# A hybrid diffusion layer: the FFN's up projection with both halves of its input in one 512-column operand

## The chip, the cores and the metric

The kernel runs on one core of a Trainium2 chip. The metric is the device time of one execution in microseconds; for the kernel before it is the median of three runs.

## The reference

One layer works on 256 latent tokens and 256 context tokens, 2048 channels wide, in fp32. The first part (modulated norm, one combined input projection, windowed attention and gated linear attention, merge, output projection) is not touched by the change. The second part is a ConvFFN with 5632 hidden channels:

```python
def conv_ffn(h, w_up, conv_w, conv_b, w_down):
    T = h.shape[1]
    u = h @ w_up
    up = jnp.pad(u, ((0, 0), (CONV_W // 2, CONV_W // 2), (0, 0)))
    u = sum(up[:, j:j + T] * conv_w[j] for j in range(CONV_W)) + conv_b
    a, g = jnp.split(u, 2, axis=-1)
    return (jax.nn.silu(a) * g) @ w_down

x = x + mod_x[5] * conv_ffn(modulate(x, g_ffn[l], mod_x[3], mod_x[4]),
                            w_up[l], conv_w[l], conv_b[l], w_down[l])
```

`mod_x[5]` is a gate row, silu(c) times a 2048 x 2048 part of `w_mod`; the kernel computes it in the background of the up projection.

## The kernel before, in words

**Products in three parts.** Every fp32 operand of a large product is split into a high part, rounded to fp32r (`whi`, `h2h`, `ah`), and the rest (`wlo`, `h2l`, `al`). A product is the sum of three: high x high, high x low and low x high, all added up in one PSUM region. `split` (L60) does it with an ACT copy (L61) and a DVE subtraction (L62).

**Weights.** They come in blocks of 256 rows x 512 columns (two k tiles of 128), loaded by SP's queue into seven `raw` buffers (L152) and split into three `whi` and three `wlo` buffers (L159, L160). The split is issued at high priority, so it stands ahead of other work in the queues of ACT and DVE.

**Order.** The instructions are not run in the order in which the code emits them: a planner, when the program is built, lays out each engine's queue from priorities, buffers that come free and its own estimate of durations. On the chip each engine then works through its queue in that order.

**Up projection** (L911 to L936). The 5632 hidden channels are taken in 11 blocks of 512, six in half 0 and five in half 1; after each half the down projection takes what is there. Each block has two sides (the two halves of `w_up`'s columns), each side one `proj_T` of 8 steps of two k tiles. In a step PE does 24 matmuls of 256 columns (the tokens): with weights `whi` 16, each column tile and k tile once with `h2h` (L203) and once with `h2l` (L206), and with `wlo` 8 with `h2h` (L203 again). Two column tiles share a bank, so a side takes two of the four banks of the pool `acc`, and the next side the other two. At the end of a side `up_evac` reads the banks: ACT scales by the middle tap and adds the bias (L923), DVE adds the two neighbours' taps (L924, L926), straight out of PSUM; side 0 goes through silu (L929), side 1 is multiplied with it (L931) and split into `ah` and `al` for the down projection.

**The input** `h2h`, `h2l` is made just before: per k tile DVE scales `x1T` (L376), ACT adds the shift and rounds (L377), DVE subtracts (L378).

**The other four banks** are the pool `ps`: one `main` and three `side`. Transposes and small products elsewhere in the kernel use them.

**Background work.** `tick()` runs at the head of each step of a projection. It counts down deferred work (`defer(n, fn)`: fn is emitted at the first tick at which its count falls below zero) and runs background steps at a rate: in half 0 it is 0.36 steps a tick, 32 steps in all. Each is two DVE multiply-adds of a `w_mod` block into `macc` (L264, L266); its block shares the seven `raw` buffers and SP's queue with the weights. Every eighth step ends a sum: a transpose and a reduction on DVE (L270, L272), then, deferred by three ticks, a little matmul `pcl` into the `main` bank (L276), copies out of it and the bias (L280, L282) into `gcol2`. After half 0's blocks `rows_from_cols` turns `gcol2` into the gate row: a PE transpose (L291), an ACT copy, a store to DRAM and a load spread over all partitions (L297, POOL's queue).

**Down projection** (`proj_nat`, L941 to L953): per 512 output columns the two token tiles are the stationary operands and the weights move, 512 columns a matmul (L176, L177, L181); `dn_evac` multiplies with the gate row (L945) and adds.

Of the kernel before, what the change touches and what calls it, by code (L numbers as in the profile page):

```python
# [8 lines left out]
F32 = mybir.dt.float32  # L9
F32R = mybir.dt.float32r  # L10
# [6 lines left out]
P = 128  # L17
# [13 lines left out]
def layer_kernel(ctx, tc, A, out):  # L31
# [18 lines left out]
    def M(name, shape, dt=F32):  # L50
        return big.tile(shape, dt, name=name, tag="M")
# [4 lines left out]
    def bank(name, shape=(P, 512), side=False):  # L56

        return ps.tile(list(shape), F32, name=name, tag="side" if side else "main", bufs=3 if side else 1)
# [66 lines left out]
    def defer(n, fn):  # L125

        later.append([n, fn])

    def flush():
        while later:  # L130
            later.pop(0)[1]()

    def tick():

        for e in later:
            e[0] -= 1
        while later and later[0][0] < 0:
            later.pop(0)[1]()
        if beside:
            beside[2] += beside[1]  # L140
            while beside[2] >= 1.0:
                beside[2] -= 1.0
                next(beside[0], None)
        bg_rate[1] += bg_rate[0]
        while bg_rate[1] >= 1.0 and bg_steps:
            bg_rate[1] -= 1.0
            bg_steps.pop(0)()
# [37 lines left out]
    def proj_T(w, c0, kts, rhs, evac):  # L185

        n = len(rhs)
        per = 2 // n
        banks = [acc.tile([P, 512], F32, name="acc", tag="acc") for _ in range(4 // per)]
        for k0 in kts[::2]:  # L190
            tick()
            nk = min(2, kts[-1] + 1 - k0)
            hi, lo = wsplit(w[k0 * P:(k0 + nk) * P, c0:c0 + 512])
            for part in range(2):
                for f in range(4):
                    for k in range(nk):
                        kt = k0 + k
                        w_ = (lo if part else hi)[:, k, f * P:(f + 1) * P]
                        for i, r in enumerate(rhs):
                            b = (f % per) if n == 1 else i  # L200
                            o = banks[f // per][:, b * T:(b + 1) * T]
                            ahi, alo = r(kt)
                            PE.matmul(o, w_, ahi, start=(kt == kts[0] and b == 0 and part == 0),  # L203
                                      stop=(kt == kts[-1] and part == 1), skip_group_check=True)
                            if part == 0:
                                PE.matmul(o, w_, alo, start=False, stop=False, skip_group_check=True)  # L206
        for i in range(len(banks)):
            evac(i, banks[i])

    ALL = list(range(KT))  # L210


# [26 lines left out]

        return [lambda k0=k0: step(k0) for k0 in range(0, KT, nk)]  # L240

    def mod_latent(parts):


        seq = [(part, dst, j, k0) for part, dst in parts for j in range(4) for k0 in range(0, KT, 2)]
        raws, a = {}, []

        def get(i):
            if i < len(seq) and i not in raws:
                part, _, j, k0 = seq[i]  # L250
                c0 = part * D + j * 512
                raws[i] = wload(w_mod[k0 * P:k0 * P + 256, c0:c0 + 512])

        def step(i):
            part, dst, j, k0 = seq[i]
            get(i)
            get(i + 1)
            if k0 == 0:
                a[:] = [W2("mod", "macc", [P, 512])]
            raw = raws[i]  # L260
            for k in range(2):
                kt = k0 + k
                if kt == 0:
                    V.tensor_scalar(a[0], raw[:, 0, :], ccol[:, 0:1], None, op0=ALU.mult)  # L264
                else:
                    V.scalar_tensor_tensor(a[0], raw[:, k, :], ccol[:, kt:kt + 1], a[0],  # L266
                                           op0=ALU.mult, op1=ALU.add)
            if k0 == KT - 2:
                tr = W2("mod", "mtr", [P, 16, 32])
                V.transpose(tr.rearrange("p a c -> p (a c)"), a[0])  # L270
                rs = sm.tile([P, 16], F32, name="mrs", tag="mrs", bufs=2)
                V.tensor_reduce(rs, tr, op=ALU.add, axis=AX.X)  # L272

                def out():
                    pc = bank("pcl", (32, 16))
                    PE.matmul(pc, sel[:, 0:32], rs, start=True, stop=True)  # L276
                    pv = pc.rearrange("p (a b) -> p b a", b=4)
                    d = dst[:, 4 * j:4 * j + 4]
                    for b4 in range(4):
                        V.tensor_copy(d[32 * b4:32 * b4 + 32, :], pv[:, b4, :])  # L280
                    b0 = part * 16 + j * 4
                    V.tensor_tensor(d, d, bmod[:, b0:b0 + 4], op=ALU.add)  # L282

                defer(3, out)

        return [lambda i=i: step(i) for i in range(len(seq))]

# [86 lines left out]
    def affine_split(hi, lo, xk, row, scale, shift):  # L374

        V.scalar_tensor_tensor(xk, xk, scale, row, op0=ALU.mult, op1=ALU.mult)  # L376
        S.activation(hi, xk, AF.Identity, bias=shift)  # L377
        V.scalar_tensor_tensor(lo, xk, shift, hi.bitcast(F32), op0=ALU.add, op1=ALU.subtract)  # L378
# [518 lines left out]
    r1 = rms_scale(s1, D, [P, 2])  # L897
    V.scalar_tensor_tensor(scale2, scale2, 1.0, gffn, op0=ALU.add, op1=ALU.mult)
    rrow = token_rows("fb", "rrow", r1)
    h2h = [M(f"h2h{i}", [P, 8, T], F32R) for i in range(2)]  # L900
    h2l = [M(f"h2l{i}", [P, 8, T], F32R) for i in range(2)]
    for kt in range(KT):
        xk = x1T[kt // 8][:, kt % 8, :]
        affine_split(h2h[kt // 8][:, kt % 8, :], h2l[kt // 8][:, kt % 8, :], xk, rrow,
                     scale2[:, kt:kt + 1], shift2[:, kt:kt + 1])
    bg_steps.extend(mod_latent([(5, gcol2)]))
    bg_rate[:] = [0.36, 0.0]
    h2 = [lambda kt: (h2h[kt // 8][:, kt % 8, :], h2l[kt // 8][:, kt % 8, :])]

    w_up, w_down = A["w_up"][0], A["w_down"][0]  # L910
    for half, blocks in enumerate((range(0, 6), range(6, 11))):  # L911
        n = len(blocks)
        ah = [M("ah", [P, 8, T], F32R) for _ in range((n + 1) // 2)]
        al = [M("al", [P, 8, T], F32R) for _ in range((n + 1) // 2)]
        for i, j in enumerate(blocks):
            u = [[W2("fc", "u", [P, 2, T]) for _ in range(2)] for _ in range(2)]

            def up_evac(p_, b, side, j=j, u=u, i=i, ah=ah, al=al):
                uu = u[side][p_]
                for f in range(2):  # L920
                    fi = side * 44 + j * 4 + 2 * p_ + f
                    d, bf = uu[:, f, :], b[:, f * T:(f + 1) * T]
                    S.activation(d, bf, AF.Identity, scale=cw1[:, fi:fi + 1], bias=cb[:, fi:fi + 1])  # L923
                    V.scalar_tensor_tensor(d[:, 1:T], bf[:, 0:T - 1], cw0[:, fi:fi + 1], d[:, 1:T],  # L924
                                           op0=ALU.mult, op1=ALU.add)
                    V.scalar_tensor_tensor(d[:, 0:T - 1], bf[:, 1:T], cw2[:, fi:fi + 1], d[:, 0:T - 1],  # L926
                                           op0=ALU.mult, op1=ALU.add)
                if side == 0:
                    S.activation(uu, uu, AF.Silu)  # L929
                else:  # L930
                    V.tensor_tensor(uu, uu, u[0][p_], op=ALU.mult)  # L931
                    q = slice((i % 2) * 4 + 2 * p_, (i % 2) * 4 + 2 * p_ + 2)
                    split(ah[i // 2][:, q, :], al[i // 2][:, q, :], uu)

            proj_T(w_up, j * 512, ALL, h2, lambda p_, b: up_evac(p_, b, 0))
            proj_T(w_up, DFF + j * 512, ALL, h2, lambda p_, b: up_evac(p_, b, 1))  # L936
        if half == 0:
            assert not bg_steps
            flush()
            gate2 = rows_from_cols("gate2", gcol2)  # L940
        for j in range(4):  # L941
            def dn_evac(t, b, j=j, half=half, gate2=gate2):
                js = slice(j * 512, (j + 1) * 512)
                y = W2("fc", "yd", [P, 512])
                V.tensor_tensor(y, b, gate2[:, js], op=ALU.mult)  # L945
                if half == 0:
                    V.tensor_tensor(x1[t][:, js], x1[t][:, js], y, op=ALU.add)
                else:
                    V.tensor_tensor(y, x1[t][:, js], y, op=ALU.add)
                    nc.sync.dma_start(out[0, t * P:(t + 1) * P, js], y)  # L950

            proj_nat(w_down, blocks[0] * 512, j * 512, list(range(n * 4)), [tok(ah, al, 0), tok(ah, al, 1)],
                     dn_evac)  # L953
# [52 lines left out]
```

## Time and profile before

| | |
|---|---|
| median of 3 runs | 2056.09 us (2054.43 to 2057.13) |
| the profiled execution | 2061.47 us, of which the span of instructions 2059.7 us |
| mean granted TensorE clock | 0.989 |
| up projection, half 0 | about 1301 to 1584 us of the span |
| down projection, half 0 | about 1584 to 1715 us |
| up projection, half 1 | about 1715 to 1945 us |
| down projection, half 1, and end | about 1945 to 2060 us |

PE is the matmul unit, PEld its weight loads (which overlap matmuls), DVE, ACT and POOL the vector, scalar and general engines, SP the engine whose queue issues the loads. A row of the timeline gives the start in us, the duration, engine, line, operation and, in brackets, the idle time before it with what ended it. A group's row gives busy time and the mean of one in ns, then the idle time before. A row of waits gives total us, times, and the longest. A window's row gives the busy us of each engine in a stretch.

### The profile page before, as it was taken

The numbers are of one execution on the slowest core, as the hardware profiler recorded it, in microseconds if no ns is written. First come the engines' busy times: TensorE is split into PE (matmuls) and PEld (weight loads), VectorE is DVE, ScalarE is ACT, GpSimd is POOL, SyncE is SP. The second block draws the span as 40 slices with busy tenths as digits, with TensorE's granted clock in tenths as the row PEclk, the third lists the DMA queues.
The fourth block names the chain that finished last, engine by engine and source line by source line (L and its number), as shares of the span: only waits on it lengthen the run. The fifth ranks groups of instructions, "written<-read, shape, count | busy, mean of one in ns | idle before, by whom it ended". The sixth has DMA issues, their size and how long they took to land.

```text
span 2059.7 us, 30028 instructions
## 1 busy us (share of the span) xinstructions
PE 1998.4 (97%) x11792; PEld 1727.0 (84%) x11792; DVE 1399.2 (68%) x2149; ACT 932.7 (45%) x1306; POOL 38.9 (2%) x62
## 2 busy tenths in 40 slices
PE   6999999999999999999999999899999999999998
PEld 4778888888787777788788888899999889999987
DVE  4657577887758888777776455877787455556654
ACT  4323464552345665444344444544445334445532
POOL 0001000001000000000000000000000000000000
PEclk8999999999999999999999999899999999999999
DMA  9977322346553466788886766576776666666563
GB/s 346 360 261 217 95 82 83 92 134 203 162 153 113 135 194 198 254 274 273 275 267 218 230 211 205 177 252 226 235 260 208 201 192 191 182 182 183 184 214 112
DMA packets 214350, 413.71 MB, mean 201 GB/s; under 512 B 12548, under 2 KB 21092, under 8 KB 213184
## 3 DMA queue, kind: packets, MB, share of 16 engines
q1 hardware_dynamic: 212320, 406.89, 62.0%
q0 software_dynamic: 1360, 4.74, 0.8%
q8 instruction: 92, 1.51, 0.3%
q14 instruction: 50, 0.41, 0.1%
q10 hardware_dynamic: 528, 0.17, 0.0%
HBM read 409.63 MB, written 2.11 MB: 200 GB/s over the span
## 4 chain that ended last, share of the span: by engine, by line
PE 78%; DVE 9%; DMA 8%; ACT 2%; issue 2%; DVEq 0%; POOL 0%; ACTq 0%; SPq 0%
PE acc L203 20%; PE acc L176 13%; PE acc L177 13%; PE acc L181 13%; PE acc L206 10%; DMA raw<-in_w_mod 8%; DVE wlo L62 3%; DVE macc L266 3%; PE pm L227 1%; PE pa L534 1%; PE po L620 1%; ACT whi L61 1%; PE pa L599 1%; PE ptp L776 1%; PE poa L782 0%
## 5 line engine op out<-in xcount | busy, mean ns | idle before, releaser
L61 ACT ACTIVATE whi<-raw 128x1024 fp32r<-128x1024 f32 x568 | 601.0, 1060 | 833.9 <-PE acc L177 512.4
L62 DVE TENSOR_TENSOR wlo<-raw,whi 128x1024 fp32r<-128x1024 f32 x568 | 693.9, 1226 | 359.6 <-ACT whi L61 327.0
L203 PE MATMUL acc<-h2h,whi 128*128 128x256 f32 x1408 | 347.4, 284 | 1.5 <-ACT h2h L377 1.5
L206 PE MATMUL acc<-h2l,whi 128*128 128x256 f32 x1408 | 346.9, 284 | 0.0
L266 DVE SCALAR_TENSOR_TENSOR macc<-raw,ccol,macc 128x512 f32<-128x512 f32 x240 | 180.3, 751 | 137.3 <-DMA raw<-in_w_mod 133.9
L203 PEld LDWEIGHTS acc<-h2h,whi 128*128 128x128 f32 x1408 | 271.5, 193 | 2.0 <-ACT h2h L377 1.8
L206 PEld LDWEIGHTS acc<-h2l,whi 128*128 128x128 f32 x1408 | 271.4, 193 | 0.2
L203 PE MATMUL acc<-h2h,wlo 128*128 128x256 f32 x1408 | 198.5, 284 | 1.7 <-DVE wlo L62 1.7
L203 PEld LDWEIGHTS acc<-h2h,wlo 128*128 128x128 f32 x1408 | 182.4, 193 | 1.9 <-DVE wlo L62 1.9
L176 PE MATMUL acc<-whi,h00hi 128*128 128x512 f32 x352 | 141.0, 400 | 0.9 <-DVE kb L394 0.6
L176 PE MATMUL acc<-whi,h01hi 128*128 128x512 f32 x352 | 139.8, 397 | 0.0
L177 PE MATMUL acc<-whi,h00lo 128*128 128x512 f32 x352 | 139.7, 397 | 0.0
L177 PE MATMUL acc<-whi,h01lo 128*128 128x512 f32 x352 | 137.8, 391 | 0.0
L176 PE MATMUL acc<-whi,ah 128*128 128x512 f32 x352 | 137.1, 389 | 0.0
L177 PE MATMUL acc<-whi,al 128*128 128x512 f32 x352 | 137.0, 389 | 0.0
L181 PE MATMUL acc<-wlo,h00hi 128*128 128x512 f32 x352 | 98.2, 394 | 0.0
L181 PE MATMUL acc<-wlo,h01hi 128*128 128x512 f32 x352 | 96.9, 393 | 0.5 <-DVE wlo L62 0.5
L181 PE MATMUL acc<-wlo,ah 128*128 128x512 f32 x352 | 94.1, 389 | 0.0
L176 PEld LDWEIGHTS acc<-whi,h00hi 128*128 128x128 f32 x352 | 66.7, 190 | 14.7 <-ACT h00hi L377 0.7
L181 PEld LDWEIGHTS acc<-wlo,h00hi 128*128 128x128 f32 x352 | 66.1, 189 | 13.9 <-DVE wlo L62 0.3
L181 PEld LDWEIGHTS acc<-wlo,ah 128*128 128x128 f32 x352 | 66.1, 188 | 13.8
L176 PEld LDWEIGHTS acc<-whi,ah 128*128 128x128 f32 x352 | 66.1, 188 | 13.7
(369 smaller groups left out, 3267.7 us busy)
## 6 DMA issues: line engine op xcount, KB each, us to landing
raw<-in_w_in SPq DMA_DIRECT2D x208, 512.0 KB, 4.4
raw<-in_w_up SPq DMA_DIRECT2D x176, 512.0 KB, 3.9
raw<-in_w_mod SPq DMA_DIRECT2D x128, 512.0 KB, 4.2
raw<-in_w_down SPq DMA_DIRECT2D x88, 512.0 KB, 4.3
mraw<-in_w_mod SPq DMA_DIRECT2D x32, 1024.0 KB, 12.0
raw<-in_w_attn_o SPq DMA_DIRECT2D x32, 512.0 KB, 4.7
raw<-in_w_gla_o SPq DMA_DIRECT2D x32, 512.0 KB, 5.1
raw<-in_w_out SPq DMA_DIRECT2D x32, 512.0 KB, 4.1
```

Source lines behind the costliest of these rows:

```text
L61: S.activation(hi, src, AF.Copy)
L62: V.tensor_tensor(lo, src, hi.bitcast(F32), op=ALU.subtract)
L176: PE.matmul(banks[i], ahi, hi[:, k, :], start=(kt == kts[0]), stop=False)
L177: PE.matmul(banks[i], alo, hi[:, k, :], start=False, stop=False)
L181: PE.matmul(banks[i], l(kt)[0], lo[:, k, :], start=False, stop=(kt == kts[-1]))
L203: PE.matmul(o, w_, ahi, start=(kt == kts[0] and b == 0 and part == 0), stop=(kt == kts[-1] and part == 1), skip_group_check=True)
L206: PE.matmul(o, w_, alo, start=False, stop=False, skip_group_check=True)
L227: PE.matmul(a[0][q:q + 32, :], cS[:, kt, :], raw[:, k, :], start=(kt < 4), stop=(kt >= 12))
L266: V.scalar_tensor_tensor(a[0], raw[:, k, :], ccol[:, kt:kt + 1], a[0], op0=ALU.mult, op1=ALU.add)
L534: PE.matmul(pa[:, t, :], k2[:, dt, t * P:(t + 1) * P], q2[:, dt, tq * P:(tq + 1) * P], start=(dt == 0), stop=(dt == 1))
L599: PE.matmul(pa[:, t, :], kk[:, dt, t * P:(t + 1) * P], qq[:, dt, :], start=(i == 0 and dt == 0), stop=(i == 1 and dt == 1))
L620: PE.matmul(po, x_, y_[:, s, :], start=(n == 0), stop=(n == 11))
```

## The change

- The two halves of the input lie side by side: `h2` is four tiles of 4 k tiles x 2 halves x 256 tokens, so `h2[kt // 4][:, kt % 4, :, :]` is one operand of 512 columns.
- `proj_pair` takes the place of `proj_T`: with `whi` one matmul of 512 columns per column tile and k tile, into a whole bank (first half of the bank high x high, second half high x low); with `wlo` one of 256 columns into the first half. A side takes four banks, one for each column tile.
- `up_banks`: side 0 uses the four `acc` banks, side 1 the `main` and the three `side` banks.
- `up_evac` runs once for each column tile: ACT copies the second half of the bank to `us`, DVE adds the first half to it, and the taps read `us`.
- The gate's sums no longer defer themselves by three ticks: they are put on a list, which the next side 0 defers by three ticks, or which is emptied after the last block of half 0.

```diff
+    def proj_pair(w, c0, kts, pair, banks, evac):
+        for k0 in kts[::2]:
+            tick()
+            nk = min(2, kts[-1] + 1 - k0)
+            hi, lo = wsplit(w[k0 * P:(k0 + nk) * P, c0:c0 + 512])
+            for f in range(4):
+                for k in range(nk):
+                    PE.matmul(banks[f], hi[:, k, f * P:(f + 1) * P], pair(k0 + k),
+                              start=(k0 + k == kts[0]), stop=False, skip_group_check=True)
+            for f in range(4):
+                for k in range(nk):
+                    PE.matmul(banks[f][:, 0:T], lo[:, k, f * P:(f + 1) * P], pair(k0 + k)[:, 0, :],
+                              start=False, stop=(k0 + k == kts[-1]), skip_group_check=True)
+        for f in range(4):
+            evac(f, banks[f])
...
-    def mod_latent(parts):
+    def mod_latent(parts, put=lambda fn: defer(3, fn)):
...
-                defer(3, out)
+                put(out)
...
-    h2h = [M(f"h2h{i}", [P, 8, T], F32R) for i in range(2)]
-    h2l = [M(f"h2l{i}", [P, 8, T], F32R) for i in range(2)]
+    h2 = [M(f"h2{i}", [P, 4, 2, T], F32R) for i in range(4)]
     for kt in range(KT):
         xk = x1T[kt // 8][:, kt % 8, :]
-        affine_split(h2h[kt // 8][:, kt % 8, :], h2l[kt // 8][:, kt % 8, :], xk, rrow,
+        affine_split(h2[kt // 4][:, kt % 4, 0, :], h2[kt // 4][:, kt % 4, 1, :], xk, rrow,
                      scale2[:, kt:kt + 1], shift2[:, kt:kt + 1])
-    bg_steps.extend(mod_latent([(5, gcol2)]))
+    sums = []
+    bg_steps.extend(mod_latent([(5, gcol2)], sums.append))
     bg_rate[:] = [0.36, 0.0]
...
+    def up_banks(side):
+        if side == 0:
+            while sums:
+                defer(3, sums.pop(0))
+            return [acc.tile([P, 512], F32, name="acc", tag="acc") for _ in range(4)]
+        return [bank("accs", side=(f > 0)) for f in range(4)]
...
-            def up_evac(p_, b, side, j=j, u=u, i=i, ah=ah, al=al):
+            def up_evac(f, b, side, j=j, u=u, i=i, ah=ah, al=al):
+                p_ = f // 2
                 uu = u[side][p_]
...
+                d = uu[:, f % 2, :]
+                fi = side * 44 + j * 4 + f
+                us = W2("fa", "us", [P, T])
+                S.activation(us, b[:, T:2 * T], AF.Copy)
+                V.tensor_tensor(us, b[:, 0:T], us, op=ALU.add)
+                S.activation(d, us, AF.Identity, scale=cw1[:, fi:fi + 1], bias=cb[:, fi:fi + 1])
+                V.scalar_tensor_tensor(d[:, 1:T], us[:, 0:T - 1], cw0[:, fi:fi + 1], d[:, 1:T],
+                                       op0=ALU.mult, op1=ALU.add)
+                V.scalar_tensor_tensor(d[:, 0:T - 1], us[:, 1:T], cw2[:, fi:fi + 1], d[:, 0:T - 1],
+                                       op0=ALU.mult, op1=ALU.add)
+                if f % 2 == 0:
+                    return
                 if side == 0:
                     S.activation(uu, uu, AF.Silu)
...
-            proj_T(w_up, j * 512, ALL, h2, lambda p_, b: up_evac(p_, b, 0))
-            proj_T(w_up, DFF + j * 512, ALL, h2, lambda p_, b: up_evac(p_, b, 1))
+            for side in range(2):
+                proj_pair(w_up, side * DFF + j * 512, ALL, lambda kt: h2[kt // 4][:, kt % 4, :, :],
+                          up_banks(side), lambda f, b, side=side: up_evac(f, b, side))
         if half == 0:
             assert not bg_steps
+            while sums:
+                sums.pop(0)()
             flush()
```

More of the change, by code (lines that the diff above doesn't have):

```diff
@@ L899, in layer_kernel @@
     rrow = token_rows("fb", "rrow", r1)
-    h2h = [M(f"h2h{i}", [P, 8, T], F32R) for i in range(2)]
-    h2l = [M(f"h2l{i}", [P, 8, T], F32R) for i in range(2)]
+    h2 = [M(f"h2{i}", [P, 4, 2, T], F32R) for i in range(4)]
     for kt in range(KT):
         xk = x1T[kt // 8][:, kt % 8, :]
-        affine_split(h2h[kt // 8][:, kt % 8, :], h2l[kt // 8][:, kt % 8, :], xk, rrow,
+        affine_split(h2[kt // 4][:, kt % 4, 0, :], h2[kt // 4][:, kt % 4, 1, :], xk, rrow,
                      scale2[:, kt:kt + 1], shift2[:, kt:kt + 1])
-    bg_steps.extend(mod_latent([(5, gcol2)]))
+    sums = []
+    bg_steps.extend(mod_latent([(5, gcol2)], sums.append))
     bg_rate[:] = [0.36, 0.0]
-    h2 = [lambda kt: (h2h[kt // 8][:, kt % 8, :], h2l[kt // 8][:, kt % 8, :])]
+    def up_banks(side):
[4 more added lines that the diff above has]
+        return [bank("accs", side=(f > 0)) for f in range(4)]
     w_up, w_down = A["w_up"][0], A["w_down"][0]
@@ L916, in layer_kernel @@
             u = [[W2("fc", "u", [P, 2, T]) for _ in range(2)] for _ in range(2)]
-            def up_evac(p_, b, side, j=j, u=u, i=i, ah=ah, al=al):
+            def up_evac(f, b, side, j=j, u=u, i=i, ah=ah, al=al):
+                p_ = f // 2
                 uu = u[side][p_]
[L920 to L927, printed above, removed]
+                d = uu[:, f % 2, :]
[10 more added lines that the diff above has]
+                    return
                 if side == 0:
```

## The prediction

> **What bounds the kernel now.** I read the engine totals first, then the chain that ended last, then busy time by stage, in windows cut at the borders of the up projection (half 0: 1301 to 1584, half 1: 1714.8 to 1945) and the down projection.
>
> ```profile
> PE 1998.4 (97%) x11792; PEld 1727.0 (84%) x11792; DVE 1399.2 (68%) x2149; ACT 932.7 (45%) x1306; POOL 38.9 (2%) x62
> ...
> PE 78%; DVE 9%; DMA 8%; ACT 2%; issue 2%; DVEq 0%; POOL 0%; ACTq 0%; SPq 0%
> ```
>
> ```profile
> core 0: us, PE busy (x) PEld busy (x) DVE busy (x) ACT busy (x) POOL busy (x), PEclk, DMA share, GB/s
> 1301.00:1584.00 283.00, 280.89 (x2312) 279.90 (x2313) 215.75 (x318) 140.81 (x179) 0.00 (x0) 0.99 0.71 227
> 1584.00:1716.00 132.00, 132.00 (x590) 109.48 (x590) 73.16 (x74) 54.31 (x56) 1.06 (x2) 1.00 0.63 201
> 1716.00:1946.00 230.00, 230.00 (x1916) 229.87 (x1915) 137.33 (x172) 110.99 (x136) 0.00 (x0) 1.00 0.62 184
> ```
>
> In both halves PE is busy all the time at full clock; DVE is at 76% in half 0 and 60% in half 1, ACT at half. So the stage is worth what PE's own issue of matmuls costs, as long as DVE and ACT keep up. How PE spends one step (two k tiles) shows in the timeline, for the up projection and, with 512-column matmuls, for the down projection:
>
> ```profile
> 1578.32 0.28 PE L203 MATMUL acc<-h2h,whi 128*128 128x256 f32 x1
> ...
> 1580.24 1.12 PE L203 MATMUL acc<-h2h,wlo 128*128 128x256 f32 x8
> ...
> 1581.20 0.28 PE L203 MATMUL acc<-h2h,whi 128*128 128x256 f32 x1
> ```
>
> ```profile
> 1600.56 0.39 PE L176 MATMUL acc<-whi,ah 128*128 128x512 f32 x1
> ...
> 1602.38 1.07 PE L181 MATMUL acc<-wlo,ah 128*128 128x512 f32 x4
> 1603.28 0.39 PE L176 MATMUL acc<-whi,ah 128*128 128x512 f32 x1
> ```
>
> The 0.28 and 0.39 us of single matmuls overlap; what counts is start to start. An up step takes 1581.20 - 1578.32 = 2.88 us for 24 narrow matmuls, 0.120 us each. A down step takes 1603.28 - 1600.56 = 2.72 us for 12 wide ones, 0.2267 us each. Twice the columns cost 0.1067 us more, so a matmul has a fixed part of about 0.0133 us beside its columns.
>
> **The change, part by part.**
>
> *Joined operand.* The product of the weight's high part with both halves of the input goes from 16 narrow matmuls to 8 wide ones; the low part's 8 narrow matmuls stay. By the two pitches a step becomes 8 x 0.2267 + 8 x 0.120 = 2.773 us: 0.107 us less, eight fixed parts. There are 11 blocks x 2 sides x 8 steps = 176 steps: 18.8 us less, 10.2 of them in half 0 (96 steps) and 8.5 in half 1 (80). The columns streamed are the same, so this is all there is to win on PE: 0.9% of the kernel.
>
> The Trainium skill (TensorE: Matmul & The Clock Gate, section Back-to-back issue gap) gives a warm matmul N/2.4 + 2.5 ns. By that a step would go from 24 x 109.2 to 8 x 215.8 + 8 x 109.2 ns, 20 ns less, and the whole gain would be an estimated 3.5 us. This trace does not agree: 120 and 227 ns in these fp32r streams, each matmul with its own weight load, so I go by the rows.
>
> *Start of the stage.*
>
> ```profile
> 1301.37 0.79 PE L203 MATMUL acc<-h2h,whi 128*128 128x256 f32 x2 [1.53 <-ACT h2h L377]
> 1301.48 1.27 DVE L378 SCALAR_TENSOR_TENSOR h2l<-x1T,shift,h2h 128x256 fp32r<-128x256 f32 x3
> ...
> 1302.01 0.58 PE L206 MATMUL acc<-h2l,whi 128*128 128x256 f32 x1
> ```
>
> Now PE starts when the high half of k tile 0 is there; a joined operand needs the low half too, as the first L206 does: 1302.01 - 1301.37 = +0.6 us, once.
>
> *Reading the banks.* Each of the 88 column tiles gets an ACT copy of the second half-bank and a DVE add of the first; the conv instructions then read the sum from SBUF, where the bank was read before. The copy and the add are not in the trace; the nearest rows are a 256-column copy out of a bank, a 256-column DVE add, and the instructions that they stand with:
>
> ```profile
> L329 ACT ACTIVATE rrow<-pr x3: 383/383/383, 18.4 to 1299.9; 128x256 f32<-128x256 f32 x3
> ```
>
> ```profile
> L924 DVE SCALAR_TENSOR_TENSOR u<-acc,cw,u 128x255 f32<-128x255 f32 x88 | 38.3, 476 | 0.0
> ...
> L931 DVE TENSOR_TENSOR u<-u 128x512 f32<-128x512 f32 x22 | 14.2, 686 | 0.0
> ...
> L565 DVE TENSOR_TENSOR segs<-segs 128x256 f32<-128x256 f32 x32 | 13.4, 420 | 1.2 <-ACT q L552 1.2
> ```
>
> That is 88 x 0.383 = 34 us more on ACT and 88 x 0.42 = 37 us more on DVE. In half 1 (40 tiles) DVE goes from 137 to 154 us of about 221, ACT from 111 to 126: hidden under PE, cost nothing. In half 0 (48 tiles) ACT goes to 159 of 273, but DVE to 215.75 + 20.2 = 236 of 273, and there DVE also waits:
>
> ```profile
> DVE macc L266 <- DMA raw<-in_w_mod: 40.4, 15, 4.5
> ...
> DVE macc L264 <- DMA raw<-in_w_mod: 3.5, 2, 2.9
> ```
>
> ```profile
> 1470.15 1.54 DVE L266 SCALAR_TENSOR_TENSOR macc<-raw,ccol,macc 128x512 f32<-128x512 f32 x2 [4.52 <-DMA raw<-in_w_mod]
> 1471.60 2.35 DVE L62 TENSOR_TENSOR wlo<-raw,whi 128x1024 fp32r<-128x1024 f32 x2
> ...
> 1472.88 1.22 PE L203 MATMUL acc<-h2h,wlo 128*128 128x256 f32 x8 [1.74 <-DVE wlo L62]
> ...
> 1475.17 1.02 ACT L923 ACTIVATE u<-acc,cb,cw 128x256 f32<-128x256 f32 x2 [5.82 <-DVE u L926]
> ```
>
> The gate's background sum (macc) sits in DVE's queue and waits for w_mod for 43.9 us in all; behind it wait the weight's low part (wlo) and the conv. Once it reached PE, for 1.74 us; an ACT wait of 5.82 us right behind it did not. So PE has some 5 us of cover per event, three weight buffers deep. If these waits stayed whole, half 0 would need 215.75 + 20.2 + 43.9 = 279.8 us of DVE against 272.8 of PE: +7.0 us. If they shrink as DVE has more to do before each (a load not waited for is not late), nothing is lost, and the 1.7 us stall may go too: -1.7. I take +3, nearer the middle since a 7 us cut in 43.9 is enough, but the waits sit in lumps of up to 4.5 us.
>
> *Two bank sets.* Side 0 takes the four acc banks, side 1 the other four. Each set is read while the other side's 8 steps (22 us) run; four tiles take DVE 4 x (0.42 + 2 x 0.476) = 5.5 us, so in the steady blocks no bank is late: nothing. Once, at the start of half 1, side 0 wants all four acc banks, the last two of which hold the end of the down projection:
>
> ```profile
> 1714.55 0.69 DVE L945 TENSOR_TENSOR yd<-acc,gate 128x512 f32<-128x512 f32 x1 [0.85 <-PE acc L181]
> 1714.80 0.28 PE L203 MATMUL acc<-h2h,whi 128*128 128x256 f32 x1
> ...
> 1716.93 0.69 DVE L945 TENSOR_TENSOR yd<-acc,gate 128x512 f32<-128x512 f32 x1
> ```
>
> The fourth bank is wanted six wide matmuls in, 1714.80 + 1.36 = 1716.16, and its yd ends at 1717.62: up to +1.5 us, 0 if DVE's order changes; I take +1.
>
> *The gate's sums.* Their little matmul (pcl) uses a bank that side 1 now holds, so it moves to the next side 0. The first three of four are free there. The last background step falls on tick 32/0.36 = 89, the first of block 5's side 1, after the last side 0; so the fourth sum now comes after the stage, behind the reading of side 1's first bank, and the gate's transpose behind it. In PE's order stand then pcl, a DVE wait, the transpose, and the down projection.
>
> ```profile
> 541.85 1.12 PE L711 MATMUL ptk<-ident,sq 128*128 128x128 f32 x4 [5.01 <-DVE sq L700]
> ...
> 813.64 0.39 PE L181 MATMUL acc<-wlo,h00hi 128*128 128x512 f32 x1
> 813.87 0.60 PE L816 MATMUL pto<-ident,sr 128*128 128x128 f32 x4
> 814.23 0.94 PE L181 MATMUL acc<-wlo,h00hi 128*128 128x512 f32 x3
> ...
> 1584.08 0.27 PE L291 MATMUL pt_gate<-ident,gcol 128*16 128x128 f32 x1
> ```
>
> Deferred transposes are put between other matmuls (here inside one step's four), so the order is planned, and ready matmuls may go first; but a plan that is early costs 5.01 us, as at 541.85. Cost: 0 if planned late; if left in place, what stands ahead in DVE's queue: 5.5 us for the four tiles, 4 x 0.686 for the products and splits, up to three wlo: 5.5 + 2.7 + 3 x 1.2 = 12 us. I take +1, as the deferred transposes of the trace mostly wait for nothing. The gate rows themselves have time:
>
> ```profile
> L945 DVE TENSOR_TENSOR yd<-acc,gate x16: 680/688/692, 1616.6 to 2054.4; 128x512 f32<-128x512 f32 x16
> ```
>
> ```profile
> DMA to landing us min/median/max: 6.8/6.9/6.9
> ```
>
> Their first reader is 1616.6 - 1584.1 = 32 us behind the transpose, and their last load lands in 6.9.
>
> *Sum:* -18.8 + 0.6 + 3 + 1 + 1 = -13.2 us. The profiled execution took 2061.5 us (span 2059.7 and 1.8 around it), 5.4 above the median of the runs; 2061.5 - 13.2 = 2048.3 for a like execution, and 2056.1 - 13.2 = 2042.9 for the median, which I predict: 2043.
>
> **Rivals**, all against the median.
>
> 1. *DVE becomes the bound of half 0.* The waits for w_mod stay whole, half 0 takes 279.8 instead of 272.8 us. For it: 4.5 us waits with wlo behind them. Against: they need shrink only by a sixth. Sum -18.8 + 0.6 + 7 + 1 + 1 = -9.2: 2047; with lumps that add to it, 2050.
> 2. *PE waits at the end of half 0* for the late gate sum, 12 us instead of 1: -2.2, 2054. For it the 5.01 us case, against it the transposes planned late.
> 3. *A wide matmul costs nearly two narrow ones here*, 0.240 us: the fixed part then is no saving, a step stays at 2.88 us, and only the costs remain: +4 to +5.6, 2060 to 2062. The down projection's 0.2267 speaks against it. (By the skill's gap the gain of 3.5 us would leave 2058.)
> 4. *Slower: the reading becomes a ladder between ACT and DVE.* Copy (ACT), add (DVE), scale (ACT), two taps (DVE), silu: in-order queues that also carry whi and wlo. Each of the 88 tiles adds one more handover in each direction; if DVE or ACT stand still there, whi comes late and PE stops. The 16.2 us left when the rest costs 2.6 are eaten when PE loses 16.2/88 = 0.18 us per tile, 0.74 us in each of the 22 readings. At 1.3 us a reading: +12, 2068. For it: the 5.82 us wait of ACT on DVE. Against: it did not reach PE, and half 1 has DVE at 70% and no such waits.
>
> **How the numbers follow.** My forecast (2036 to 2046) 0.60, rival 1 0.14, rival 2 0.06, rival 3 0.07, rival 4 0.13. Within 0.2% (4.1 us, about what a measurement of this kernel can tell from no change) lie rival 2 and most of rival 3; faster are forecast and rival 1: 0.74; slower rival 4 and a part of 3: 0.14; same 0.12. The low end is the full saving with no cost but the start, and the 1.7 us stall gone: 2056.1 - 18.8 + 0.6 - 1.7 = 2036. The high end takes in rivals 1 and 2: 2056; I set 2057, leaving out 0.2.
>
> **What the changed profile would show.** Wide matmuls start to start 0.227 us and steps of 2.77 us in half 1 (80 steps, 222 us): else the first term is wrong. PE's waits for wlo in half 0 above some 5 us in sum: DVE is the bound there. A gap on PE at the end of half 0 ahead of pcl or pt_gate: rival 2. PE waits spread over all 22 readings, in half 1 too: rival 4. DVE's added time should be near 37 us and ACT's near 34. I am wrong most easily by the new order of ACT and DVE, which no row of before shows.

## The result, and the profile after

The changed kernel takes 2039.18 us (median of 4 runs, 2037.73 to 2041.93) where the kernel before takes 2056.61 (4 runs): a ratio of 0.9921, 95% interval 0.9908 to 0.9933, 17.4 us less. A second set of runs gave 0.9909 (0.9893 to 0.9925). The forecast was 2043, 13.2 us less.

The page's engine totals and its chain after:

```profile
PE 1979.4 (97%) x10384; PEld 1647.3 (81%) x10384; DVE 1430.0 (70%) x2237; ACT 960.7 (47%) x1394; POOL 38.9 (2%) x62
...
PE 78%; DVE 10%; DMA 8%; ACT 2%; issue 2%; DVEq 0%; POOL 0%; ACTq 0%; SPq 0%
```

PE has 1408 matmuls fewer (8 in each of 176 steps), DVE 31 us more work, ACT 28 us, and PE still leads the chain. The windows of both halves of the up projection, with the down projection between them:

```profile
core 0: us, PE busy (x) PEld busy (x) DVE busy (x) ACT busy (x) POOL busy (x), PEclk, DMA share, GB/s
1296.50:1569.00 272.50, 272.35 (x1545) 239.15 (x1546) 230.27 (x356) 153.83 (x223) 0.00 (x0) 0.99 0.72 236
1569.00:1701.00 132.00, 131.85 (x583) 108.64 (x582) 74.90 (x83) 55.21 (x59) 1.06 (x2) 1.00 0.60 201
1701.00:1923.00 222.00, 222.00 (x1273) 195.31 (x1273) 148.88 (x207) 121.73 (x170) 0.00 (x0) 1.00 0.59 189
```

PE's timeline gives the exact borders: the first matmul of half 0, of its down projection, of half 1 and of the last down projection, and two steps of half 1 (a row of the timeline merges like instructions, so x8 is a run of eight).

```profile
1296.65 3.78 PE L219 MATMUL acc<-h,whi 128*128 128x512 f32 x8 [2.18 <-DVE h L396]
...
1568.49 0.40 PE L176 MATMUL acc<-whi,ah 128*128 128x512 f32 x1
...
1699.92 1.52 PE L219 MATMUL acc<-h,whi 128*128 128x512 f32 x6
1701.28 0.88 PE L223 MATMUL acc<-h,wlo 128*128 128x256 f32 x6
...
1842.36 2.00 PE L219 MATMUL acc<-h,whi 128*128 128x512 f32 x8
1844.20 1.12 PE L223 MATMUL acc<-h,wlo 128*128 128x256 f32 x8
1845.15 2.00 PE L219 MATMUL acc<-h,whi 128*128 128x512 f32 x8
...
1923.37 0.40 PE L176 MATMUL acc<-whi,ah 128*128 128x512 f32 x1
```

Before, the same four borders lay at 1301.37, 1584.10, 1714.80 and 1945.20. The two of them at the down projections are these rows:

```profile
1584.10 0.48 PE L176 MATMUL acc<-whi,ah 128*128 128x512 f32 x1
...
1945.20 0.40 PE L176 MATMUL acc<-whi,ah 128*128 128x512 f32 x1
```

So:

| stretch | before | after | difference |
|---|---|---|---|
| half 0 of the up projection | 282.73 | 271.84 | -10.9 |
| its down projection | 130.70 | 131.43 | +0.7 |
| half 1 | 230.40 | 223.45 | -6.9 |
| the rest (span less the last border) | 114.5 | 114.3 | -0.2 |

That is -17.3 us, what the medians say. The two profiled spans differ by 22.0; the other 4.7 us lie ahead of the up projection's first matmul, where the change touches nothing but the wait for its input (0.65 us longer, see below). In the executions profiled for this study that border lies anywhere from 1295.6 to 1301.4 us, so lengths of stages are compared here, not spans.

A step takes 1845.15 - 1842.36 = 2.79 us, not the forecast's 2.773: the eight narrow matmuls take 0.95 us, 0.119 each, but the eight wide ones 1.84 us, 0.230 each, where the down projection has 0.2267.

### The profile page after: what moved, and what is told of

Read it like the earlier page. It is cut to its first block, busy times and chain, and to the rows that moved or that the text cites. A ratio compares the mean times of both kernels' runs of the same rounds, so it can differ in the third digit from the quotient of the medians.

```text
span 2037.7 us, 27395 instructions
## 1 busy us (share of the span) xinstructions
PE 1979.4 (97%) x10384; PEld 1647.3 (81%) x10384; DVE 1430.0 (70%) x2237; ACT 960.7 (47%) x1394; POOL 38.9 (2%) x62
## 4 chain that ended last, share of the span: by engine, by line
PE 78%; DVE 10%; DMA 8%; ACT 2%; issue 2%; DVEq 0%; POOL 0%; ACTq 0%; SPq 0%
PE acc L176 13%; PE acc L177 13%; PE acc L181 13%; PE acc L219 8%; PE accs L219 8%; DMA raw<-in_w_mod 8%; PE acc L223 4%; PE accs L223 4%; PE acc L203 3%; DVE wlo L62 3%; DVE macc L284 3%; PE acc L206 2%; PE pm L245 1%; PE pa L552 1%; ACT whi L61 1%
## 5 line engine op out<-in xcount | busy, mean ns | idle before, releaser
L219 PE MATMUL acc<-h,whi 128*128 128x512 f32 x704 | 178.6, 396 | 2.2 <-DVE h L396 2.2
L219 PE MATMUL accs<-h,whi 128*128 128x512 f32 x704 | 176.3, 392 | 0.0
L219 PEld LDWEIGHTS acc<-h,whi 128*128 128x128 f32 x704 | 127.8, 191 | 25.6 <-DVE h L396 2.5
L219 PEld LDWEIGHTS accs<-h,whi 128*128 128x128 f32 x704 | 126.6, 189 | 22.6
L223 PEld LDWEIGHTS acc<-h,wlo 128*128 128x128 f32 x704 | 97.0, 192 | 7.1
L223 PEld LDWEIGHTS accs<-h,wlo 128*128 128x128 f32 x704 | 96.0, 190 | 6.9
L223 PE MATMUL acc<-h,wlo 128*128 128x256 f32 x704 | 99.1, 284 | 0.0
L223 PE MATMUL accs<-h,wlo 128*128 128x256 f32 x704 | 98.2, 282 | 0.0
```

The source lines that it names most:

```text
L219: PE.matmul(banks[f], hi[:, k, f * P:(f + 1) * P], pair(k0 + k), start=(k0 + k == kts[0]), stop=False, skip_group_check=True)
L223: PE.matmul(banks[f][:, 0:T], lo[:, k, f * P:(f + 1) * P], pair(k0 + k)[:, 0, :], start=False, stop=(k0 + k == kts[-1]), skip_group_check= ...
```

## The experiments

Each is an edit of the changed kernel. Where one execution was taken, stages and steps are read, not the total.

**The matmuls alone.** Everything stays but the wide matmul:

```diff
-                    PE.matmul(banks[f], hi[...], pair(k0 + k), start=(k0 + k == kts[0]), ...)
+                    for q in range(2):
+                        PE.matmul(banks[f][:, q * T:(q + 1) * T], hi[...], pair(k0 + k)[:, q, :],
+                                  start=(k0 + k == kts[0] and q == 0), ...)
```

> The changed kernel with each wide matmul of the up projection issued as two of 256 columns (high half, low half) into the same bank; bank sets, reading and deferred sums stay. If the gain is PE's matmul count: a step goes from 2.79 back to 2.88 us, half 1 (80 steps) from 223.5 to about 230.4 us, the whole kernel by 15 us to about 2054; the 2 to 3 us of the gain that are not in the steps stay. If the gain came from the bank sets, the later reading or the deferred sums: steps would not matter, and the time stays near 2039.

2055.88 us against 2057.71 (ratio 0.9991, 0.9982 to 1.0001). The borders in PE's timeline:

```profile
1298.95 3.79 PE L220 MATMUL acc<-h,whi 128*128 128x256 f32 x16 [1.53 <-ACT h L396]
...
1578.68 0.40 PE L176 MATMUL acc<-whi,ah 128*128 128x512 f32 x1
...
1710.04 1.60 PE L220 MATMUL acc<-h,whi 128*128 128x256 f32 x12
...
1940.53 0.40 PE L176 MATMUL acc<-whi,ah 128*128 128x512 f32 x1
```

Half 1 is back at 1940.53 - 1710.04 = 230.5 us, 2.88 a step, the length it had before. The joined operand is the source of half 1's gain, all of it, and the bank sets and the longer reading, taken together, neither give nor cost anything there. Half 0 takes 1578.68 - 1298.95 = 279.7 us: with the same matmuls as before it is 3.0 us shorter. That part is not the joined operand's. It is read from one execution of each kernel; the medians differ by 1.8 us, with an interval that just reaches nothing. Step by step, 2.0 of the 3.0 us are one step of the kernel before, 4.87 us long, with the 1.74 us stall behind `wlo`, which is not there any more; 0.35 is the fourth gate sum, which now comes after the half; and 0.6 lies in the first two steps, which start at a granted clock of 0.50 before and 0.53 here and get the full clock about 1.2 us sooner here. So only 2.0 us have to do with the waits.

**One bank set.**

```diff
-        return [bank("accs", side=(f > 0)) for f in range(4)]
+        return [acc.tile([P, 512], F32, name="acc", tag="acc") for _ in range(4)]
```

> The changed kernel with both sides on the four acc banks. If the second set hides the reading: PE waits at the start of each of about 20 sides until the first bank is copied and added, 1 to 3 us a side, half 1 goes from 223.5 to 233 to 253 us and the kernel to 2060 to 2100; steps away from a side's start stay at 2.79 us. If the planner finds other work or the banks come free in PE's own pace: less than 3 us in all.

One execution: 2111 us, above the 2060 to 2100 expected. Half 0 takes 315.8 us (+43.9), half 1 248.7 (+25.2, inside the range). PE's timeline at the start of a side of half 1, what PE waited for in that half (total us, times, longest), and the half's window:

```profile
1842.49 1.11 PE L223 MATMUL acc<-h,wlo 128*128 128x256 f32 x8
1845.40 1.91 PE L219 MATMUL acc<-h,whi 128*128 128x512 f32 x6 [1.79 <-DVE us L950]
```

```profile
PE acc L219 <- DVE us L950: 16.1, 9, 1.8
```

```profile
1746.40:1995.00 248.60, 230.66 (x1281) 200.88 (x1280) 153.25 (x211) 124.26 (x176) 0.00 (x0) 0.98 0.58 172
```

The last narrow run starts at 1842.49 and would end at 1843.44; the next side starts at 1845.40, 1.96 us late, behind the add. 25.2 us over 10 sides is 2.5 a side, of which this lateness is 1.96. Most of the rest goes with the granted clock, 0.98 in this half where the changed kernel has 1.00: 0.02 x 248.6 = 5.0 us, an estimate. In half 0 it is 0.95 against 0.99; why the clock was lower was not tried. Alternating sets are no gain of their own, but without them the wide form would lose far more than it wins: a side now fills all four banks.

**The reading, three times.** Two more copies and adds of each bank, results unused:

```diff
+                us2 = W2("fa", "us2", [P, 2, T])
+                for _ in range(2):
+                    S.activation(us2[:, 0, :], b[:, T:2 * T], AF.Copy)
+                    V.tensor_tensor(us2[:, 1, :], b[:, 0:T], us2[:, 0, :], op=ALU.add)
```

> The changed kernel with two more copies and adds of each bank (results unused), so the added reading is three times as large: 34 us more on ACT, 37 us more on DVE in each half in proportion. Half 1: DVE from 149 to about 182 of 223 us, no change in time (within 1 us). Half 0: DVE from 230 to about 270 of 272 us; if its waits for w_mod shrink as its own work grows, PE loses 0 to 5 us there; if they stay at their 20 us, half 0 grows by 15 to 20 us.

One execution, 2039.69 us. Half 0 takes 271.8 us, half 1 223.5: nothing is lost in either. Its windows:

```profile
1297.00:1568.90 271.90, 271.78 (x1543) 238.68 (x1544) 258.41 (x443) 178.19 (x309) 0.00 (x0) 0.99 0.76 236
1700.00:1923.50 223.50, 223.50 (x1282) 196.60 (x1281) 173.67 (x280) 141.11 (x243) 0.00 (x0) 1.00 0.63 189
```

DVE's waits for `w_mod` in half 0, in the changed kernel and with three readings:

```profile
DVE macc L284 <- DMA raw<-in_w_mod: 18.2, 10, 4.1
...
DVE macc L282 <- DMA raw<-in_w_mod: 2.5, 1, 2.5
```

```profile
DVE macc L284 <- DMA raw<-in_w_mod: 0.2, 1, 0.2
```

With DVE's work in half 0 the waits went from 43.9 us (215.8 us busy, before) to 20.7 (230.3) and 0.2 (258.4). In these plans the idle time was slack that looked like a limit: a DVE with more to do comes later to the load and finds it there. That the added work alone did this is argued, since the planner lays out the order anew for each kernel, and below are two plans in which DVE has 233 us of work and waits for `w_mod` for over 100. (I had expected 270 us of DVE; the 96 more adds filled 28.1 us, 0.29 each, where one lasts 0.42: neighbours overlap.)

**What a narrow matmul costs.** The low part's 256-column matmul as two of 128, and then with 64 of the 128 stationary columns (half of the low part left out):

```diff
-                    PE.matmul(banks[f][:, 0:T], lo[:, k, f * P:(f + 1) * P], pair(k0 + k)[:, 0, :], ...)
+                    for q in range(2):
+                        PE.matmul(banks[f][:, q * P:(q + 1) * P], lo[:, k, f * P:(f + 1) * P],
+                                  pair(k0 + k)[:, 0, q * P:(q + 1) * P], ...)
```

```diff
+                        PE.matmul(banks[f][0:64, q * P:(q + 1) * P], lo[:, k, f * P:f * P + 64],
+                                  pair(k0 + k)[:, 0, q * P:(q + 1) * P], ...)
```

> The changed kernel with each 256-column matmul of the weight's low part issued as two of 128 columns. If a matmul costs a fixed 13 ns beside its columns, a 128-column one takes 53 + 13 = 67 ns, a step grows by 16 x 0.067 - 8 x 0.12 = 0.11 us and the kernel by 19 us to about 2058. If narrow matmuls are bound by PE's issue of the pair of weight load and matmul, 0.12 us whatever the width, a step grows by 0.96 us and the kernel by about 169 us to 2208.

> The changed kernel with each matmul of the weight's low part replaced by two of 128 columns whose stationary operand has 64 columns in place of 128 (half of the low part's product is left out). If narrow matmuls are bound by the number of pairs of weight load and matmul that PE issues: 0.11 us each, as with 128 stationary columns, and a time near 2220. If the weight load's own length bounds them (its 128 columns): 0.06 to 0.07 us each, a step of about 2.9 us, a time near 2060.

One execution each, 2219.75 and 2148.5 us. A step of half 1 with 128 stationary columns, then with 64:

```profile
1899.56 2.07 PE L219 MATMUL accs<-h,whi 128*128 128x512 f32 x8
1901.47 1.90 PE L224 MATMUL accs<-h,wlo 128*128 128x128 f32 x16
1903.20 2.07 PE L219 MATMUL accs<-h,whi 128*128 128x512 f32 x8
```

```profile
1900.73 2.06 PE L219 MATMUL acc<-h,whi 128*128 128x512 f32 x8
1902.63 1.12 PE L224 MATMUL acc<-h,wlo 128*64 128x128 f32 x16
1903.59 2.06 PE L219 MATMUL acc<-h,whi 128*128 128x512 f32 x8
```

With 128 columns moving a matmul takes (1903.20 - 1901.47)/16 = 0.108 us on the mean (the second starts 0.06 after the first, the others every 0.111), not the 0.067 of a fixed part beside the columns: that reading of the two pitches does not carry below 256 columns. With half the stationary columns it is (1903.59 - 1902.63)/16 = 0.060. The number of pairs of weight load and matmul is the same in both, so the count does not bound them; the number of stationary columns does. Whether it does so through the load or through the half as many output rows, these two runs do not separate. The Trainium skill (TensorE: Matmul & The Clock Gate, section LDWEIGHTS (loading the stationary operand)) gives a load of P columns P/1.2 ns, an estimate of 107 and 53 ns. The 128-column run agrees within 5%: its loads start every 0.111 us, although the row of one load lasts 0.19. The other does not contradict it: its loads start every 0.060 us, and by the first pitches (0.1067 us for 256 columns more) its 128 moving columns alone would need about 0.053.

The wide matmuls behind these runs take 0.239 and 0.238 us on the mean of eight, most of the excess in the first of them. Both totals are far above what half 1 says: half 0 took 383.2 and 371.3 us, where 96 steps of half 1's kind (3.64 and 2.86 us) would be about 350 and 275. There DVE's queue did become the bound, though DVE is busy for only 233 us: the waits for `w_mod` reach PE through `wlo`. The granted clock is lower there too, 0.98 and 0.93. With 64 columns, DVE's waits up to 1575 us of the span, and PE's in the whole half:

```profile
DVE macc L286 <- DMA raw<-in_w_mod: 81.3, 20, 6.8
```

```profile
PE acc L224 <- DVE wlo L62: 34.4, 19, 3.6
PE accs L224 <- DVE wlo L62: 29.3, 14, 3.6
```

So the mechanism of rival 1 exists in another plan of the same stage. Why these plans put the sums ahead of their loads was not tried.

**All wide, and alternating.** The low part's matmul with 512 columns (it adds low x low), and, in another kernel, each narrow matmul directly behind its wide one:

```diff
-                    PE.matmul(banks[f][:, 0:T], lo[...], pair(k0 + k)[:, 0, :], ...)
+                    PE.matmul(banks[f], lo[...], pair(k0 + k), ...)
```

```diff
                     PE.matmul(banks[f], hi[...], pair(k0 + k), ...)
-            for f in range(4):
-                for k in range(nk):
                     PE.matmul(banks[f][:, 0:T], lo[...], pair(k0 + k)[:, 0, :], ...)
```

> The changed kernel with the low part's matmuls 512 columns wide too (this adds the product of the two low parts, which the others leave out). If the wide ones' 0.230 us comes from the narrow run ahead of them: 16 x 0.2267 = 3.63 us a step, 0.833 us more, about 2186. If this stage's wide matmuls take 0.230 us by themselves: 3.69 us a step, about 2197.

> The changed kernel with the order of a step altered: each wide matmul is followed at once by the narrow one of the same column tile, instead of eight wide and then eight narrow. If the 26 ns a step that the wide ones lose come from the run of narrow ones ahead of them: a step goes from 2.794 to 8 x 0.2267 + 8 x 0.12 = 2.774 us, 3.5 us off the kernel, about 2036. If each switch from narrow to wide costs its 7 to 9 ns: eight switches a step, 2.83 to 2.85 us, 6 to 9 us more, 2045 to 2048.

> The changed kernel once more, beside the alternating one on the same chip: 2039, ratio to before 0.992.

All wide, one execution, 2184.87 us; a step of half 1:

```profile
1851.19 1.98 PE L219 MATMUL acc<-h,whi 128*128 128x512 f32 x8
1853.00 1.98 PE L223 MATMUL acc<-h,wlo 128*128 128x512 f32 x8
1854.81 1.98 PE L219 MATMUL acc<-h,whi 128*128 128x512 f32 x8
```

3.62 us for 16, 0.226 each: this stage's wide matmuls are as fast as the down projection's when no narrow run stands ahead of them. Alternating, the borders of half 1:

```profile
1703.06 0.39 PE L219 MATMUL acc<-h,whi 128*128 128x512 f32 x1
...
1924.98 0.39 PE L176 MATMUL acc<-whi,ah 128*128 128x512 f32 x1
```

221.9 us over 80 steps, 2.774 a step: the forecast's sum of the two pitches. So the 0.02 us a step missing from the forecast are the price of the narrow run for the wide ones behind it: nothing without one, 0.004 us a wide matmul behind 8 narrow ones, 0.011 to 0.012 behind 16 of 128 columns (each the mean of eight). That the weight loads fall behind in the run would fit, and is argued only.

In total the alternating kernel took 2043.62 us (ratio 0.9935, 0.9922 to 0.9948), the changed one beside it 2039.22. The profiled execution, 2041.07 us, is the fastest of its six; what the others lose beyond its stages no trace shows. In it half 0 was 274.7 us, 2.8 longer, with PE waits for the low part of the weight, which is wanted 1.6 us earlier in each step:

```profile
PE accs L221 <- DVE wlo L62: 0.7, 1, 0.7
```

But most of the loss is in PE's own pitch. Two steps of half 0, each from its first wide matmul to the next step's:

```profile
1341.20 0.40 PE L219 MATMUL accs<-h,whi 128*128 128x512 f32 x1
...
1343.97 0.40 PE L219 MATMUL acc<-h,whi 128*128 128x512 f32 x1
...
1375.10 0.40 PE L219 MATMUL accs<-h,whi 128*128 128x512 f32 x1
...
1377.93 0.40 PE L219 MATMUL accs<-h,whi 128*128 128x512 f32 x1
```

The first takes 2.77 us, as nearly all steps do up to 1347 us, from 1538 on and in half 1. From 1347 to 1535 us nearly every step takes 2.83, with the same matmuls and no wait inside. This slower pattern begins behind a matmul that DVE's `wlo` made 0.1 us late and ends behind a gate sum's little matmul. Against the changed kernel's 2.793 us, some 64 x 0.034 = 2.2 us are lost by it, and 1.0 by the wait at 1521. So both step times that the expectation names occur, in one run; what keeps the slower pattern going was not tried.

**Alternating in half 1 only**, the version that these two point to:

```diff
-                          up_banks(side), lambda f, b, side=side: up_evac(f, b, side))
+                          up_banks(side), lambda f, b, side=side: up_evac(f, b, side), half == 1)
```

> The changed kernel with the alternating order in half 1 only, where DVE has time, and eight and eight in half 0. If half 0's loss with the alternating order is DVE's (the low part of the weight is wanted earlier there) and half 1's gain is PE's: half 0 271.9 us as in the changed kernel, half 1 221.9, the kernel 1.5 us below it, about 2037.7: less than the runs can tell in the total, to be read in the stages. If half 0 loses again, the loss was not DVE's.

2038.92 us (ratio 0.9914, 0.9900 to 0.9929). In PE's timeline:

```profile
1569.53 0.40 PE L176 MATMUL acc<-whi,ah 128*128 128x512 f32 x1
...
1700.96 0.39 PE L219 MATMUL acc<-h,whi 128*128 128x512 f32 x1
...
1922.87 0.39 PE L176 MATMUL acc<-whi,ah 128*128 128x512 f32 x1
```

Half 1 takes 221.9 us, half 0 (from 1297.75) 271.8: both as expected, 1.6 us less in sum, which the totals cannot tell from nothing. Half 0's loss belongs to the alternating order there. DVE's lateness sets it off, but most of it is lost in PE's steps of 2.83 us, not in waits for DVE.

## Why the prediction was right, and where it was off

- *Joined operand, -18.8.* Right in kind, too large: a step went from 2.880 to 2.793 us, 0.087 x 176 = 15.3 us, and with narrow matmuls put back, 15 us return (7.0 in half 1, 7.9 in half 0). The term missed that eight wide matmuls behind eight narrow ones take 0.230 us, not 0.2267: 0.02 x 176 = 3.5 us. Its reading of a fixed part per matmul is a line through two widths, 256 and 512, and does not carry to 128. By the gap between matmuls that the Trainium skill states (TensorE: Matmul & The Clock Gate, section Back-to-back issue gap; N/2.4 + 2.5 ns, which the section calls the isolated gap), an estimate of 1408 x 2.5 ns = 3.5 us of gain would have been all; half 1 alone gave 6.9, so the runs go against it here.
- *Start, +0.6.* PE waits 2.18 us for the low half of the first k tile where it waited 1.53 for the high half: +0.65, as said. It lies ahead of the first matmul, so the table does not have it.
- *Waits in half 0, +3.* Wrong in sign. The waits for `w_mod` were halved, not carried over, and the stall that reached PE (1.74 us) is gone with its step's 2.0 us; the rest of the 3.0 us at equal matmuls is not this term's. The bound below nothing (-1.7) was nearer than the value taken. The term added DVE's new work to its old idle time, although that idle time was only waiting for loads and could shrink. Which part of the change took the stall away, the reading, the bank sets or the new plan, was not separated.
- *Last two banks of half 1, +1.* Nothing: the plan runs six wide and six narrow matmuls of the first three banks ahead of the fourth (1699.92 and 1701.28 above).
- *The gate's last sum, +1.* The plan puts it between the down projection's matmuls, as for the other transposes:

```profile
1570.34 0.39 PE L181 MATMUL acc<-wlo,ah 128*128 128x512 f32 x1
1570.65 0.24 PE L294 MATMUL pcl<-mrs,sel 128*32 128x16 f32 x2
1570.82 0.97 PE L181 MATMUL acc<-wlo,ah 128*128 128x512 f32 x3
...
1582.52 0.39 PE L176 MATMUL acc<-whi,ah 128*128 128x512 f32 x1
1583.05 0.27 PE L309 MATMUL pt_gate<-ident,gcol 128*16 128x128 f32 x1
1583.07 0.47 PE L177 MATMUL acc<-whi,al 128*128 128x512 f32 x1
```

  The down projection is 0.7 us longer by them; that work stood in half 0 or at its end before, so little is new.
- *Reading hidden.* Right, with room: three times as much costs nothing. The copy took 0.38 us and the add 0.42, as the rows of before said. The busy totals rose by 28 us on ACT and 31 on DVE, not by 34 and 37, since neighbouring instructions overlap: the durations, summed, rose by 37 and 38, and 3 of ACT's are the slower scale and bias of the last section.
- *Rivals.* 1: not in this plan; in two others the waits for `w_mod` did reach PE. 2: no wait. 3: no, 0.230 against 0.240. 4: ACT waits for the add, but PE never: in half 1 nothing is lost against the old length at equal matmuls.

So two errors partly cancelled: 3.5 us too much gain from the steps, some 7 us too much cost (5 in the waits, 2 in the two terms of +1). That the time lies well inside the range owes something to this luck: with the gain as measured and the costs as forecast the sum would have been 2056.1 - 15.3 + 5.6 = 2046.4.

## What to carry to other kernels

Where PE's own stream is the bound, count matmuls as well as columns: two of 256 columns with the same weights cost 11 to 13 ns more than one of 512 here, and a matmul of only 128 moving columns still took 0.11 us with 128 stationary columns of fp32r. Reading sums out of twice as many banks is paid by engines with slack, and only with a second set of banks for the next block to fill. An engine's idle time behind a load is not work: before adding it to a new load, ask whether the wait would still be there if the engine came later. A new plan can also turn it into a real one, as in the two kernels whose half 0 took 371 us and more, so it has to be read again in each profile.

## What the runs showed of the hardware that was not expected

- A matmul of 128 moving columns took 0.108 us on the mean with 128 stationary columns, and 0.060 with 64.
- Wide matmuls behind a run of narrow ones are slower by 4 ns (8 of 256 columns ahead) to 12 ns (16 of 128), each the mean of eight. Alternating order took that back in half 1 (2.774 us a step), but the same stream also ran at 2.83 us a step for most of half 0.
- ACT's scale and bias of 256 columns took longer from SBUF than out of PSUM, 587 against 554 ns; the group before (busy us, mean ns of one), then the same step's row in the changed kernel (min/median/max ns):

```profile
L923 ACT ACTIVATE u<-acc,cb,cw 128x256 f32<-128x256 f32 x88 | 44.4, 554 | 23.1 <-DVE u L926 23.1
```

```profile
L951 ACT ACTIVATE u<-us,cb,cw x88: 582/587/603, 1323.8 to 1927.7; 128x256 f32<-128x256 f32 x88
```
